# Later scores and per-token-tile round trips in a two-layer decoder trunk, with more transposes taken off TensorE

## The chip, the cores and the metric

The kernel runs on one core of one Trainium2 chip. The metric is device time in microseconds (us). The kernel before takes 1003.44 us, the median of three runs (997.42, 1003.44 and 1008.15). The engines are named as in the profile: PE is TensorE's matmul side and PEld its weight load, DVE is VectorE, ACT is ScalarE, POOL is GpSimd and SP is SyncE. SP and POOL issue most of the DMAs here: SP loads the weights, POOL moves activations out to HBM and back.

## The reference

Two layers on one sequence of 256 tokens and a width of 2048. Each layer normalises x, projects it to q, k, v and a gate z, runs 16 heads' worth of attention in four groups, multiplies by silu(z), projects back and adds x. A last RMSNorm follows.

```python
def _layer_ab(x, norm_g, w_in, w_out, lam_vec, subln_g, layer_idx, pos):
    h = jnp.matmul(_rmsnorm(x, norm_g).astype(x.dtype), w_in).astype(jnp.float32)
...
    ya = _dilated_mixture(_rope(_heads(aq, A_HEADS), pos), _rope(_heads(ak, A_HEADS), pos), _heads(av, A_HEADS))
...
    yb = _diff_attention(bq[:, :, 0], bq[:, :, 1], bk[:, :, 0], bk[:, :, 1], bv, lam)
    yb = _rmsnorm(yb, subln_g) * (1.0 - lam_init)
...
    y = jnp.concatenate([ya, yb], axis=-1) * jax.nn.silu(z)
    return x + jnp.matmul(y.astype(x.dtype), w_out)

def _layer_c(x, norm_g, w_in, w_out, pos):
    h = jnp.matmul(_rmsnorm(x, norm_g).astype(x.dtype), w_in).astype(jnp.float32)
    cq, ck, cv, z = jnp.split(h, [C_WIDTH, 2 * C_WIDTH, 3 * C_WIDTH], axis=-1)
    yc = _moba_attention(_rope(_heads(cq, C_HEADS), pos), _rope(_heads(ck, C_HEADS), pos), _heads(cv, C_HEADS))
    y = _merge(yc) * jax.nn.silu(z)
    return x + jnp.matmul(y.astype(x.dtype), w_out)
```

At 256 tokens the second layer's block attention is plain causal attention. In the first layer, groups 0 and 1 are dilated attention (four heads each) and groups 2 and 3 are differential attention (two heads each, with two score maps and a value width of 256).

## The kernel before, in words

**Tiling.** The tokens are two tiles of 128. Every projection is cut into chunks of 512 output columns: 20 chunks a layer, 40 in all, in the order v q k z for group 0, then q k z v for groups 1 to 3, then four output chunks o. A chunk sums over 16 tiles of the contraction; one such step is called a slot, so a chunk has 16 slots and the kernel 640. In a slot each token tile gets three matmuls of 128x512 in a split-fp32 form: with x and w each cut into a high and a low part, high by high, high by low and low by high (`mm3`, L310). That is six matmuls a slot.

**Feeding.** SP loads the weights 1 MB at a time (four slots, three buffers). For every two slots ACT writes the weights' high part (`wh`, L122) and DVE the low part (`wl`, L123), three pairs ahead and into four buffers. ACT, DVE and POOL each work through their own list in order.

**What lies between the slots.** `at(slot, f, ...)` hangs a piece of work behind a slot's matmuls; the slot numbers are written by hand. A scheduler then orders each engine's list by these priorities and its own times, so the lists can differ a little from the numbers. `nxt` is the slot at which the chunk in question ends.

**Turning.** q, k and the gate come out of a projection as tokens by features and are needed as features by tokens. `evac_rope` (rotary for q and k, five DVE instructions) or `evac_z` works on one token tile; `turn` (L233) transposes 32x32 blocks on DVE; `place` (L238), once both token tiles are turned, stores the 512 KB tile `bz` to HBM (`dt`) and loads it back with eight DMAs (`q`, `k` or `u`), which puts the blocks in place. All of this is on POOL's queue. `split_rope` (L278) then makes the high and low parts, with ACT and DVE (`qh`, `ql`, `kh`, `kl`).

**Attention.** `softmax` (L314) makes scores for a head (`ps_s`), from k, q and their parts. `attn_t` transposes the probabilities the same way over HBM: a store `d` and four loads `p`, on POOL. `attn_h` splits them (`th`, `tl`), and `attn_o` or `diff_o` multiplies by v (`po`, `pdo`). For differential heads `diff_y` transposes the result `yb` on PE (`ps_yt`). `finish_y` multiplies by the gate and splits y (`yh`, `yl`), which the output chunks need.

**Between the layers.** After each output chunk of layer 0, `next_x` (L434) transposes the four 128-wide pieces of the new x on PE (`ps_xt`) and `split_x` splits them for layer 1.

## Time and profile before

| What | Value |
|---|---|
| median of three runs | 1003.44 us |
| profiled execution, whole | 999.49 us |
| its span, first to last instruction | 997.7 us |
| mean granted clock of TensorE | 0.971 |
| PE busy | 942.4 us (94%) |
| DVE busy | 643.0 us (64%) |
| ACT busy | 474.5 us (48%) |
| POOL busy | 200.5 us (20%) |
| PE waiting for k to come back from HBM | 41.6 us, 7 times |

PE's busy time counts pipelined matmuls from start to end, so it is not a measure of full speed; a 128x512 matmul is listed at about 0.39 us, while in a steady stretch one starts every 0.227 us. "Waits" name the engine that waited, what it was about to do, and what ended the wait. The granted clock of a stretch is 1.00 at full speed and 0.50 at half.

### The profile page before, as it was taken

The page shows a single profiled execution, that of the slowest core. Times are in us where ns is not written, and L with a number is a line of the kernel's source. Part 1 is how long each engine was busy: PE and PEld are TensorE (multiplying, and loading weights), DVE is VectorE, ACT ScalarE, POOL GpSimd, SP SyncE. Part 2 cuts the span into 40 slices and gives each one's busy share as a digit, 9 for nine tenths or more (in the row PEclk, how much of TensorE's full clock was granted, in tenths as well). Part 3 has the DMA queues.
Part 4 walks back from the last instruction along what each step waited for, and adds up shares of the span by engine and source line. Part 5 has one row for each costly group of instructions (what it writes and reads, how often), then busy time and mean ns, then how long its engine had stood idle before and what let it go on. Part 6 is the DMA issues. An engine that isn't in the chain of part 4 may idle for free. (4 is left out here: it accounts for less than half of the span.)

```text
span 997.7 us, 11928 instructions
## 1 busy us (share of the span) xinstructions
PE 942.4 (94%) x4276; PEld 778.8 (78%) x4276; DVE 643.0 (64%) x999; ACT 474.5 (48%) x711; POOL 200.5 (20%) x368
## 2 busy tenths in 40 slices
PE   8999997999799988999999999979996999799996
PEld 7887886888688867888888878868885888587886
DVE  6666875756566666665555768747664766575572
ACT  7534643553355335554554454535442644264451
POOL 0021441321113110300000125215011421132000
PEclk9999999999989998999999999989997999899999
DMA  9786776566645664655555668667665756676542
GB/s 329 259 320 232 242 241 212 198 210 244 214 161 210 213 232 137 220 196 174 187 193 185 237 212 266 219 199 234 212 209 180 245 198 211 211 241 227 187 169 84
DMA packets 42827, 213.21 MB, mean 214 GB/s; under 512 B 9040, under 2 KB 9808, under 8 KB 22672
## 3 DMA queue, kind: packets, MB, share of 16 engines
q1 hardware_dynamic: 27504, 175.21, 50.1%
q0 software_dynamic: 14976, 36.20, 11.4%
q10 hardware_dynamic: 288, 1.05, 0.3%
q8 instruction: 33, 0.54, 0.2%
q14 instruction: 26, 0.21, 0.1%
HBM read 192.23 MB, written 20.19 MB: 213 GB/s over the span
## 5 line engine op out<-in xcount | busy, mean ns | idle before, releaser
L312 PE MATMUL acc<-wh,x 128*128 128x512 f32 x2048 | 655.1, 397 | 1.6 <-ACT wh L119 1.6
L123 DVE TENSOR_TENSOR wl<-raw,wh 128x1024 fp32r<-128x1024 f32 x314 | 382.7, 1220 | 206.1 <-ACT wh L122 205.3
L122 ACT ACTIVATE wh<-raw 128x1024 fp32r<-128x1024 f32 x314 | 332.0, 1059 | 359.8 <-PE acc L312 322.2
L312 PEld LDWEIGHTS acc<-wh,x 128*128 128x128 f32 x2048 | 390.7, 191 | 81.9 <-ACT wh L119 1.8
L312 PE MATMUL acc<-wl,x 128*128 128x512 f32 x1024 | 405.1, 396 | 0.2 <-DVE wl L120 0.2
L312 PEld LDWEIGHTS acc<-wl,x 128*128 128x128 f32 x1024 | 196.0, 191 | 39.8 <-DVE wl L120 0.5
L312 PE MATMUL acc<-wh,yh 128*128 128x512 f32 x224 | 88.3, 394 | 0.0
L312 PE MATMUL acc<-wl,yh 128*128 128x512 f32 x224 | 87.4, 390 | 0.0
L312 PE MATMUL acc<-wh,yl 128*128 128x512 f32 x224 | 87.3, 390 | 0.0
L243 POOL DMA_DIRECT2D dt<-bz x24 | 13.6, 568 | 305.6 <-DVE bz L235 302.1
L360 POOL DMA_DIRECT2D p<-d x112 | 61.2, 554 | 56.8 <-DMA d<-bt 29.5
L317 PE MATMUL ps_s<-k,q 128*128 128x128 f32 x64 | 14.7, 315 | 41.8 <-DMA k<-dt 41.6
L317 PEld LDWEIGHTS ps_s<-k,q 128*128 128x128 f32 x64 | 12.8, 214 | 47.0 <-issue 29.8
L312 PEld LDWEIGHTS acc<-wh,yl 128*128 128x128 f32 x224 | 42.0, 188 | 9.1 <-DVE yl L389 0.3
L312 PEld LDWEIGHTS acc<-wl,yh 128*128 128x128 f32 x224 | 42.1, 188 | 8.4
L312 PEld LDWEIGHTS acc<-wh,yh 128*128 128x128 f32 x224 | 42.1, 188 | 8.2
L247 POOL DMA_DIRECT2D q<-dt x64 | 34.7, 550 | 39.2 <-ACT wh L122 19.7
L247 POOL DMA_DIRECT2D k<-dt x64 | 34.7, 549 | 32.6 <-DMA dt<-bz 19.6
L356 POOL DMA_DIRECT2D d<-bt x28 | 15.7, 561 | 124.3 <-DVE st L328 85.6
L247 POOL DMA_DIRECT2D u<-dt x64 | 34.7, 549 | 19.0 <-DMA p<-d 13.2
L286 DVE TENSOR_TENSOR kl<-k,kh 128x512 fp32r<-128x512 f32 x16 | 11.0, 688 | 39.1 <-ACT kh L285 39.1
L285 ACT ACTIVATE kh<-k 128x512 fp32r<-128x512 f32 x16 | 10.0, 624 | 44.3 <-DMA k<-dt 44.2
(122 smaller groups left out, 663.8 us busy)
## 6 DMA issues: line engine op xcount, KB each, us to landing
raw<-in_w SPq DMA_DIRECT2D x124, 1024.0 KB, 5.2
raw<-in_o SPq DMA_DIRECT2D x32, 1024.0 KB, 4.8
dt<-bz POOLq DMA_DIRECT2D x24, 512.0 KB, 4.2
d<-bt POOLq DMA_DIRECT2D x28, 192.0 KB, 4.3
p<-d POOLq DMA_DIRECT2D x112, 48.0 KB, 4.7
q<-dt POOLq DMA_DIRECT2D x64, 64.0 KB, 3.6
k<-dt POOLq DMA_DIRECT2D x64, 64.0 KB, 6.2
u<-dt POOLq DMA_DIRECT2D x64, 64.0 KB, 4.6
```

The lines of the kernel that those rows point to most:

```text
L122: nc.scalar.activation(ht, r, AF.Copy)
L123: nc.vector.tensor_sub(lt, r, ht.bitcast(F32))
L243: nc.gpsimd.dma_start(d, bt.rearrange("p c t h j -> p c (t h j)"))
L247: nc.gpsimd.dma_start(t[32 * c:32 * c + 32, tt].rearrange("p a h j -> p a (h j)"), dv[c, tt])
L285: nc.scalar.activation(a, v, AF.Copy)
L286: nc.vector.tensor_sub(b, v, a.bitcast(F32))
L312: nc.tensor.matmul(out_, l, r, start=start and i == 0, stop=stop and i == 2)
L317: nc.tensor.matmul(ps[:, 0:P], q[:, h * P:(h + 1) * P], k[:, 0, :, h], start=True, stop=True)
L356: nc.gpsimd.dma_start(d, bt.rearrange("p c b j -> p c (b j)"))
L360: nc.gpsimd.dma_start(pt[32 * c:32 * c + 32], dv[c])
```

## The change

Five edits.

1. **By token tile.** `turn` and `place` become one function. Each token tile's turned block is stored by itself (256 KB instead of 512 KB, a `bz` of half the size with two buffers, `dt` with four), as soon as it is turned. With the second one, the eight loads are issued: four for the first token tile, four for the second. The second token tile's rotary or gate work hangs one slot after the first's instead of two.
2. **Later scores.** `split_rope` moves from `nxt + 13` to `nxt + 18`; the first scores move from `nxt + 14` to `nxt + 22`, or to `nxt + 20` in a layer's last group. What follows them moves too; the distance between a head's scores and its product with v becomes shorter.
3. **x of layer 1.** For the first three output chunks of layer 0, `turn_x` and `turned_x` take the same way over DVE, HBM and POOL in place of `next_x`; the last output chunk keeps PE.
4. **y of the third group.** In group 2 of layer 0, `yb` is turned the same way; group 3 keeps PE.
5. **Start.** 13 instead of 10 warm-up matmuls ahead of the first weights.

```diff
-WARM = 10
+WARM = 13
...
+    def turn(src, box, tt, name, into=None):
+        n = src.shape[1]
+        bt = work.tile([P, n], F32, tag="bz", name="bz", bufs=2).rearrange("p (c h j) -> p c h j", c=4, j=32)
+        nc.vector.transpose(bt.rearrange("p c h j -> p h c j"), src.rearrange("p (h c j) -> p h c j", c=4, j=32))
+        d = dram.tile([P, 4, n // 4], F32, tag="dt", name="dt", bufs=4)
+        nc.gpsimd.dma_start(d, bt.rearrange("p c h j -> p c (h j)"))
+        box[tt] = d.rearrange("(a i) c x -> c i a x", a=4)
+        if tt == 1:
+            t = work.tile([P, 2, CW], F32, tag=name, name=name) if into is None else into
+            box["t"] = t = t.rearrange("p t (a h j) -> p t a h j", a=4, j=32)
+            for i in range(2):
+                for c in range(4):
+                    nc.gpsimd.dma_start(t[32 * c:32 * c + 32, i].rearrange("p a h j -> p a (h j)"), box[i][c])
...
+        if g < 3:
+            for tt in range(2):
+                turn(yb[:, tt], box, tt, None, yb)
...
+    def turn_x(n, box, tt):
+        turn(x_sb[:, tt, n * CW:(n + 1) * CW], box, tt, "qk"[n % 2])
+
+    def turned_x(n, h, box):
+        kt = 4 * n + h
+        split_x(1, kt, box["t"][:, :, :, h], xhl[kt].rearrange("p b (t a j) -> p b t a j", t=2, a=4))
...
-                    at(nxt + 2 * tt, evac_rope, ps, kind, (Q, K)[kind == "k"], layer, g, tt, box)
+                    at(nxt + tt, evac_rope, ps, kind, (Q, K)[kind == "k"], layer, g, tt, box)
...
-                at(nxt + 13, split_rope, kind, (Q, K)[kind == "k"], layer, g, box)
+                at(nxt + 18, split_rope, kind, (Q, K)[kind == "k"], layer, g, box)
...
+            late = g == 3
+            first = nxt + (20 if late else 22)
...
-                    at(nxt + 14 + 3 * h, attn_s, layer, g, h, md if layer == 0 else mc, box)
-                    at(nxt + 17 + 3 * h, attn_t, box)
-                    at(nxt + 32 + 2 * h, attn_h, box)
-                    at(nxt + 34 + 2 * h, attn_o, layer, g, h, box)
+                    at(first + 3 * h, attn_s, layer, g, h, md if layer == 0 else mc, box)
+                    at(first + 3 + 3 * h, attn_t, box)
+                    at(first + (13 if late else 15) + 3 * h, attn_h, box)
+                    at(first + (15 if late else 17) + 3 * h, attn_o, layer, g, h, box)
...
+            if layer == 0 and g < 3:
+                box = {}
+                for tt in range(2):
+                    at(nxt + 1 + tt, turn_x, g, box, tt)
+                for h in range(4):
+                    at(nxt + 18 + h, turned_x, g, h, box)
+            elif layer == 0:
```

The differential heads' slots change likewise: their first scores stand at `first` and `first + 5`, and their products with v at `first + 16` and `first + 30` in group 2 and at `first + 16` and `first + 21` in group 3.

How the lists move is shown for group 1 of layer 0. First PE's list around that group's first scores, before: `acc_1330` is the z chunk that follows the k chunk, x_101 is the first tile of the contraction and x_115 and x_116 are its last two, so the first scores stand behind the fifteenth slot of the z chunk.

```order
L312 MATMUL acc_1330<-wh_1425,x_115 128x512 x2
L312 MATMUL acc_1330<-wl_1426,x_115 128x512
L312 MATMUL acc_1330<-wh_1425,x_115 128x512
L317 MATMUL ps_s<-k,q 128x128
L312 MATMUL acc_1330<-wh_1425,x_116 128x512
L312 MATMUL acc_1330<-wl_1426,x_116 128x512
```

Now the same place on PE after the change: `acc_1511` is the next chunk (v), and here x_104 is the first tile of the contraction, so x_110 is its seventh.

```order
L307 MATMUL acc_1511<-wh_1512,x_110 128x512
L312 MATMUL ps_s<-k,q 128x128
L307 MATMUL ps_s<-kh,qh 128x256
L307 MATMUL ps_s<-kl,qh 128x256
L307 MATMUL ps_s<-kh,ql 128x256
L307 MATMUL acc_1511<-wh_1512,x_111 128x512
```

The first scores moved from behind slot 15 after the k chunk's end to behind slot 23, and a head's four products now stand together.

POOL's list for the same group before (q, k and gate round trips, then the four heads' probabilities):

```order
L247 DMA q<-dt 32x4x128 x8
L243 DMA dt<-bz 128x1024
L247 DMA k<-dt 32x4x128 x8
L356 DMA d<-bt 128x384
L243 DMA dt<-bz 128x1024
L360 DMA p<-d 32x4x96 x4
L247 DMA u<-dt 32x4x128 x8
L356 DMA d<-bt 128x384 x2
L360 DMA p<-d 32x4x96 x8
L356 DMA d<-bt 128x384
L360 DMA p<-d 32x4x96 x4
```

And after the change, from the k store on, without the fourth head's store and loads:

```order
L242 DMA dt<-bz 128x512
L249 DMA k<-dt 32x4x128 x4
L242 DMA dt<-bz 128x512
L249 DMA k<-dt 32x4x128 x4
L242 DMA dt<-bz 128x512
L249 DMA u<-dt 32x4x128
L242 DMA dt<-bz 128x512
L249 DMA u<-dt 32x4x128 x7
L351 DMA d<-bt 128x384
L355 DMA p<-d 32x4x96 x4
L351 DMA d<-bt 128x384 x2
L355 DMA p<-d 32x4x96 x8
```

The first four k loads now stand ahead of the second k store, and the gate's whole round trip stands ahead of the first head's store.

ACT's list around the splitting of k before, where `wh` rows feed two slots of PE each:

```order
L122 ACTIVATE wh_1459<-raw_1411 128x1024
L122 ACTIVATE wh_1481<-raw_1445 128x1024
L285 ACTIVATE kh<-k 128x4x128
L122 ACTIVATE wh_1514<-raw_1445 128x1024
L285 ACTIVATE kh<-k 128x4x128
```

And after, where `wh_1459` feeds the v chunk's first two slots and `wh_1493` its fifth and sixth:

```order
L122 ACTIVATE wh_1443<-raw_1390 128x1024
L280 ACTIVATE kh<-k 128x4x128
L122 ACTIVATE wh_1459<-raw_1429 128x1024
L122 ACTIVATE wh_1477<-raw_1429 128x1024
L280 ACTIVATE kh<-k 128x4x128
L122 ACTIVATE wh_1493<-raw_1463 128x1024
```

Counted in weight pairs, the two splits of k moved forward by three pairs and by two on ACT's list, so that they stand ahead of weights that PE needs at slot 16 and at slot 20 after the k chunk's end.

More of the change, by code (lines that the diff above doesn't have):

```diff
@@ L257, in evac_z @@
         nc.vector.scalar_tensor_tensor(z, th, 1.0, z, op0=ALU.add, op1=ALU.mult)
[L258 removed]
+        turn(z, box, tt, "u")
         if tt == 1:
[L260 removed]
+            U[layer, g] = box["t"]
     def evac_rope(ps, name, store, layer, g, tt, box):
[L263 to L264 removed]
         t1 = work.tile([P, CW], F32, tag="t1", name="rt1")
```

62 lines of the change are left out of this document (21 added, 41 removed).

## Prediction

> **What bounds the kernel now.** I read the waits of PE first, since PE is busy for 94% of the span, then the granted clock around the longest of them, then the queue that ends them. Columns of the waits: total us, times, longest.
>
> ```profile
> PE 942.4 (94%) x4276; PEld 778.8 (78%) x4276; DVE 643.0 (64%) x999; ACT 474.5 (48%) x711; POOL 200.5 (20%) x368
> PE ps_s L317 <- DMA k<-dt: 41.6, 7, 7.9
> PE ps_s L312 <- ACT kh L285: 1.8, 2, 1.6
> PE acc L312 <- ACT wh L119: 1.6, 1, 1.6
> PE po L312 <- ACT th L369: 0.5, 1, 0.5
> ```
>
> So PE loses 41.6 + 1.8 = 43.4 us in the middle of the kernel, all of it at a group's first scores; it never waits there for weights. A longer stop costs more than itself. These are stretches of PE (us, its busy time, count, granted clock, share and GB/s of DMA), each begun where PE starts again after such a wait, then two after short waits, then the start of the kernel.
>
> ```profile
> 174.25:181.00 6.75, 6.75 (x24) 0.71 0.08 20
> 274.88:281.00 6.12, 6.12 (x17) 0.53 0.01 2
> 378.04:384.00 5.96, 5.95 (x19) 0.58 0.00 0
> 664.33:671.00 6.67, 6.67 (x20) 0.60 0.04 12
> 767.36:773.00 5.64, 5.64 (x16) 0.58 0.00 0
> 868.92:875.00 6.08, 6.08 (x16) 0.54 0.00 0
> 97.00:107.00 10.00, 9.75 (x47) 1.00 0.49 171
> 592.00:600.00 8.00, 8.00 (x43) 1.00 0.33 137
> 6.60:12.00 5.40, 5.15 (x14) 0.68 1.02 335
> ```
>
> At half clock half the work is lost, so each stretch loses its length times what is missing from 1.00: 6.75 x 0.29 + 6.12 x 0.47 + 5.96 x 0.42 + 6.67 x 0.40 + 5.64 x 0.42 + 6.08 x 0.46 = 15.2 us. With the stops that makes 58.6 us of the 999.49. The two short waits were these, the first with its wait in brackets:
>
> ```profile
> 96.95 0.46 PE L317 MATMUL ps_s<-k,q 128*128 128x128 f32 x2 [1.73 <-DMA k<-dt]
> ```
>
> and the 1.6 of the row for `kh` above; neither cost any clock. The remaining time is PE at full rate, so the change is worth what it takes from these 58.6 and from PE's own list, less the new waits.
>
> Why k is late shows in one group, on PE, POOL and ACT in order of time (start, busy):
>
> ```profile
> 167.95 0.39 PE L312 MATMUL acc<-wh,x 128*128 128x512 f32 x1
> 174.25 0.55 PE L317 MATMUL ps_s<-k,q 128*128 128x128 f32 x1 [5.91 <-DMA k<-dt]
> 161.29 0.56 POOL L243 DMA_DIRECT2D dt<-bz  x1 [15.87 <-DVE bz L235]
> 165.39 4.33 POOL L247 DMA_DIRECT2D k<-dt  x8 [3.55 <-ACT wh L122]
> 187.43 0.55 POOL L243 DMA_DIRECT2D dt<-bz  x1 [1.15 <-DVE bz L235]
> 174.04 0.63 ACT L285 ACTIVATE kh<-k 128x512 fp32r<-128x512 f32 x1 [5.96 <-DMA k<-dt]
> ```
>
> PE stops at 168.2, fifteen slots after the k chunk's end. A steady matmul starts every 0.227 us (rows below), so a slot of six is 1.36 us and the chunk ended at 168.2 - 15 x 1.36 = 147.8. The store is issued 13.5 us after that, and k is there 26.2 us after it (174.04), where the scores wanted it at 20.4.
>
> **The change part by part. Later scores.** They now stand 23 slots after the chunk's end, or 21 in a layer's last group: 31.3 or 28.6 us. When is k there? DVE turns the second token tile no later than before, since its rotary work hangs one slot earlier, so I take the old 13.5 us for its store. The first four loads stand between the two stores and belong to the first; after the second store only four are left, not eight, which takes half of the 4.33 us row, 2.2 us, off the end. So k is whole at 26.2 - 2.2 = 24.0 us at the latest. Spare: 7.3 us, or 4.6 in a last group. The two waits of 43.4 us go, and with them the 15.2 us of half clock.
>
> **By token tile, store size.** DMA from issue to landing, us (median; the last rows min, median, max of p, d and of one load's issue on POOL in ns):
>
> ```profile
> dt<-bz POOLq DMA_DIRECT2D x24, 512.0 KB, 4.2
> d<-bt POOLq DMA_DIRECT2D x28, 192.0 KB, 4.3
> p<-d POOLq DMA_DIRECT2D x112, 48.0 KB, 4.7
> DMA to landing us min/median/max: 2.1/4.7/8.1
> DMA to landing us min/median/max: 2.1/4.3/6.6
> L247 POOL DMA_DIRECT2D k<-dt x64: 548/548/557, 91.6 to 866.1; - x64
> ```
>
> A store of 192 KB lands no sooner than one of 512 KB, so the halved stores gain nothing in landing and each costs one more issue of 0.56 us on POOL. The Trainium skill says otherwise ("DMA: Bandwidth & Descriptors", Anatomy of one DMA): about 2.0 us plus the bytes over 436 GB/s, by which 256 KB less would land some 0.6 us sooner, an estimate; the spare above would be 7.9 and 5.2 us and the sum the same. No run here shows that slope.
>
> **Transposes off PE.** Four of them and what they do to their neighbours:
>
> ```profile
> 436.10 0.39 PE L312 MATMUL acc<-wh,yl 128*128 128x512 f32 x1
> 436.33 0.60 PE L439 MATMUL ps_xt<-ident,x_sb 128*128 128x128 f32 x4
> 436.69 0.48 PE L312 MATMUL acc<-wh,yh 128*128 128x512 f32 x1
> 437.00 0.40 PE L312 MATMUL acc<-wl,yh 128*128 128x512 f32 x1
> ```
>
> The four take 0.36 us and the matmul after them 0.31 instead of 0.23: 0.45 us. Six calls of `next_x` and two of `diff_y` leave PE: 8 x 0.45 = 3.6 us. In return DVE gets six 128x512 and four 128x256 block transposes and POOL ten stores and forty loads. Both have room: POOL is 20% busy, and DVE idles for a third of the span. The x of the third chunk is the tight one. Its turn is issued two slots after the chunk, its loads end about 4.2 (store) + 4.4 (eight issues) + 4.7 us later, some 17 us after the chunk's end with DVE's own work, and layer 1 needs it 24 slots after (32.6 us). But ACT takes that split between two weight pairs, and the next pair is due at 18 slots, 24.5 us; four splits of 0.47 and a weight pair (both in the rows below) end near 21.6. I put nothing down for it.
>
> **Warm-up.** Ten warm-up matmuls (two passes each) end before PE's 1.6 us wait for the first weights; three more fit into it, at 3.95/10 = 0.4 us each.
>
> ```profile
> 1.06 3.95 PE L137 MATMUL pw<-ones 128*128 128x128 f32 x20 [1.06 <-DVE fs L463]
> ```
>
> The stretch from 6.6 us loses 5.40 x 0.32 = 1.7 us at half clock. Filling the pause gains between 0 and 1.7; I take 0.8.
>
> **What the change newly makes PE wait for.** Three places, since the round trips now hang more closely on what needs them. The rows: the weight splits, ACT's wait for p, the splits of p and x, and a differential head's last score and its store.
>
> ```profile
> L123 DVE TENSOR_TENSOR wl<-raw,wh 128x1024 fp32r<-128x1024 f32 x314 | 382.7, 1220 | 206.1 <-ACT wh L122 205.3
> L122 ACT ACTIVATE wh<-raw 128x1024 fp32r<-128x1024 f32 x314 | 332.0, 1059 | 359.8 <-PE acc L312 322.2 <-issue 22.7 <-DMA raw<-in_o 3.4
> ACT th L369 <- DMA p<-d: 16.0, 10, 2.7
> L369 ACT ACTIVATE th<-p 128x256 fp32r<-128x256 f32 x24 | 9.7, 405 | 8.0 <-DMA p<-d 8.0
> L370 DVE TENSOR_TENSOR tl<-p,th 128x256 fp32r<-128x256 f32 x24 | 10.1, 419 | 3.5 <-ACT th L369 3.4
> L152 ACT ACTIVATE x<-ps_xt,g_sb 128x256 fp32r<-128x256 f32 x16 | 7.5, 470 | 10.5 <-DVE x L153 7.5 <-PE ps_xt L439 2.9
> 282.79 0.29 PE L312 MATMUL ps_s<-kh,ql 128*128 128x256 f32 x1
> 289.39 0.56 POOL L356 DMA_DIRECT2D d<-bt  x1 [18.68 <-DVE bt L354]
> ```
>
> First, ACT works in order, and the second split of k now stands ahead of the weights that PE needs 20 slots after the chunk's end, 27.2 us. With k at 24.0, the split (0.63), the weight pair (1.06, 1.22) end at 26.9. It holds, by 0.3 us, on the late bound; a slow landing shows on PE. I take 0.3 us for each of eight groups, 2.4. Second, POOL's three hops. The gate's round trip is ahead of the first head's store: its store stood at 187.43, 39.6 us after the k chunk, or 31.7 without the 5.9 us stop and the 2.0 us of half clock; one slot earlier now, 4.2 to land and four loads make the first head's store leave at about 37. Store and four loads are 6.5 us, the next pair 4.3 + 4.4, the fourth store 0.6, then 4.3 + 2.2 and 4.2 to land: 26.5 us later, 63.5, plus 0.85 for the splits. Regular groups want it at 49 slots, 66.6 us: no wait. In the last group of layer 1 the list is two stores, eight loads, twice over; the third head's part is split at 58.3 us and wanted at 42 slots, 57.1: 1.3 us with the hand-over. Third, differential heads keep 14 slots (19.0 us) from the second scores to the product. The scores take about 0.5, their softmax 6.6 (282.79 to 289.39), store, loads and landing 4.3 + 2.2 + 4.2, and the splits about 1.1, an estimate for half as many columns again as in the rows: 18.9. No spare, so I take 0.6 us for three of the four heads, 1.8. Together 5.5 us. The bounds: 0.5, PE's wait for `th` before, and 8 x 2.7 = 21.6, if every group shows the longest wait of ACT for p.
>
> **The sum**, against the profiled execution: 999.5 - 43.4 - 15.2 - 3.6 - 0.8 + 5.5 = 942.0 us. The median of the runs shown is 3.9 us above that execution; the runs spread by 10.7 us, and the waits that spread go, so I don't add it.
>
> **The rivals.** *The weights become the wait.* k, x and the probabilities block ACT and DVE, which are in order, and PE stops for `wh` in every group. For: the 0.3 us above, and the 2.7. Against: DVE idles 206.1 us and ACT 359.8 in front of the weight splits, and before no such stop exists. Price: 21.6 in place of 5.5 gives 958; if in three groups it also trips the clock, at 2.5 us each (15.2/6), 966. The rows show half clock after the stop of 5.9 us and none after 1.7; between these two no row is shown. The Trainium skill ("TensorE: Matmul & The Clock Gate", Part 1) puts the window at about 3.4 us, by which most of these waits would keep the clock.
>
> *The scores still wait.* The first loads stand ahead of the second store, so a slow first landing delays it, and k with it. It would have to come 7.3 us later than reckoned. Half of the waits left, with their clock, is 29 us: 971.
>
> *Slower: POOL's hops.* If the round trips of a group take long, the fourth head is late in every group. Three hops at the longest landings (6.6 and 8.1 for 4.3 and 4.7) add 17.1 us, less 2.2 of spare (66.6 - 64.4): 14.9 a group, and 2.5 of clock, 139 us over eight groups: 1076. It turns slower than before when a group loses 57.5/8 = 7.2 us beyond the 5.5, so at about 2.3 us more on each of three hops. For: 74 more DMAs on POOL. Against: a load's issue takes 548 to 557 ns throughout, and 4.7 and 4.3 are medians over the same hops in the kernel before. The Trainium skill ("SBUF — State Buffer", "SBUF: two separate sides", the box on DVE blocking DMA) states that certain DVE instructions keep POOL from writing a DMA's descriptors; by that rule more DVE work beside more POOL DMAs would go this way. The issue row doesn't show it, with DVE 64% busy.
>
> **How the numbers follow.** The forecast has 0.73, the weights' wait 0.14, scores that still wait 0.05, slower 0.04; the other 0.04 are cases in which the gains and new waits nearly cancel. Predicted 942. The likeliest case reaches from 934 (new waits 0.5, the start's full 1.7, a lighter execution by 2) to 952; the range goes on to 962, into the first rival, and 3 us below, as landings vary from run to run. About 1% is what a measurement of this kernel can tell from no change: 993 to 1013. Faster 0.92, same 0.04, slower 0.04.
>
> **What would show it.** PE's wait for k gone or under 5 us; the mean granted clock above 0.99 instead of 0.971; no `ps_xt` behind the first three output chunks; a span near 940. The weights' rival shows as waits of PE for `wh` or `wl`, POOL's as waits of PE for `th` or `tl` behind p, the second as k in PE's waits. The forecast is wrong if any of these comes to more than 20 us.

## The result, and the profile after

The changed kernel takes 971.15 us (median of four runs, 967.66 to 975.80) against 1000.43 us for the kernel before on the same chip (997.42 to 1008.15): 0.970 of it, with an interval of 0.963 to 0.977. The profiled execution takes 967.66 us, its span 965.9 us, and the mean granted clock rose from 0.971 to 0.987. The forecast said 942.0 and reached up to 962. So the direction holds, and nearly half of the gain is missing.

First the page's row of the engines, then the waits of PE (total us, times, longest) and of ACT:

```profile
PE 931.3 (96%) x4250; PEld 771.5 (80%) x4250; DVE 648.2 (67%) x1009; ACT 468.9 (49%) x711; POOL 242.7 (25%) x442
```

```profile
PE po L307 <- ACT th L364: 8.8, 2, 6.3
PE acc L307 <- DVE wl L123: 4.2, 7, 1.2
PE ps_yt L420 <- DVE yb L407: 2.4, 1, 2.4
PE acc L307 <- ACT wh L122: 2.3, 2, 1.8
PE pdo L307 <- ACT th L364: 1.6, 2, 1.0
PE po L307 <- DVE y L381: 1.3, 1, 1.3
...
ACT kh L280 <- DMA k<-dt: 55.8, 16, 7.3
ACT th L364 <- DMA p<-d: 47.5, 16, 8.1
```

No row of PE names k any more: the 43.4 us before the first scores are gone. In their place stand six kinds of short stops. ACT, which stopped 16.0 us for p before, now stops 47.5. All pauses of PE over 0.3 us in this trace, from the end of the first chunk on, add up to 20.1 us. Four of the places are followed by half clock (stretch, PE's busy time and count, granted clock, DMA share, GB/s):

```profile
158.20:163.20 5.00, 4.98 (x14) 0.50 0.59 198
415.80:419.20 3.40, 3.40 (x10) 0.50 0.64 214
494.30:497.70 3.40, 3.40 (x10) 0.50 0.81 287
634.30:637.70 3.40, 3.40 (x12) 0.50 0.69 234
```

That is (5.0 + 3 x 3.4) x 0.5 = 7.6 us. With the forecast's other terms left as they were, 999.5 - 43.4 - 15.2 - 3.6 - 0.8 + 20.1 + 7.6 = 964.2, which is 3.5 us short of the measured 967.7. The term for new waits was 5.5 and came out at 27.7 us: 13.0 where group 0's fourth heads wait for `th` (6.28 and 2.48 us, with 2.5 and 1.7 of clock), 5.7 in layer 0's first output chunk, 5.5 behind the splits of the turned x, and 3.6 in small stops elsewhere in layer 0's group 0.

The missing 3.5 us lie behind the last matmul, where the forecast has no term: from there to the end of the span the kernel before takes 7.9 us and the changed kernel 12.1. The rows of POOL's closing instruction DRAIN give its duration in ns (shortest, median, longest of three) and when the first and the last of the three start; the longest is the first one, behind POOL's last arithmetic. Before, then after:

```profile
L630 POOLq DRAIN  x3: 40/102/3903, 991.2 to 997.4; - x3
L645 POOLq DRAIN  x3: 40/102/9945, 955.1 to 965.6; - x3
```

Before, it ended 2.7 us ahead of the span's end, and SP's wait for the output rows ended last. After, SP is through 5.1 us ahead of the end, and the closing rows of all engines start when POOL's DRAIN is over. In all 18 profiles of this case its length goes by the number of DMAs that POOL has issued: 3.90 us with 356 of them, 5.86 with 380, 7.50 with 400, 8.31 with 410 and 9.95 with 430, so about 0.082 us each. The changed kernel issues 74 more than the kernel before. Its DRAIN is 6.0 us longer, and 4.2 us of these show at the end. With these the sum is 968.4, within 1 us of the measurement.

The largest of the new waits, in three engines of the changed kernel (start, busy, in brackets the idle time before and what ended it): POOL, ACT and PE at the fourth head of group 0.

```profile
136.62 0.56 POOL L351 DMA_DIRECT2D d<-bt  x1
139.00 0.57 POOL L249 DMA_DIRECT2D q<-dt  x1 [1.82 <-ACT th L364]
...
145.82 2.18 POOL L249 DMA_DIRECT2D q<-dt  x4 [2.50 <-DMA dt<-bz]
147.99 1.09 POOL L355 DMA_DIRECT2D p<-d  x2
...
150.71 0.55 POOL L355 DMA_DIRECT2D p<-d  x1 [0.90 <-DMA q<-dt]
```

```profile
154.21 0.63 ACT L280 ACTIVATE qh<-q 128x512 fp32r<-128x512 f32 x1 [6.71 <-DMA q<-dt]
...
156.82 1.04 ACT L122 ACTIVATE wh<-raw 128x1024 fp32r<-128x1024 f32 x1
157.77 0.40 ACT L364 ACTIVATE th<-p 128x256 fp32r<-128x256 f32 x1
```

```profile
158.22 0.58 PE L307 MATMUL po<-th,vh 128*128 128x256 f32 x1 [6.28 <-ACT th L364]
```

The head's store (`d<-bt`) leaves at 136.62, but its loads (`p<-d`) only at 147.99 to 150.71: in POOL's list all eight loads of the next q stand ahead of them, and four of those wait for q's second store. The store had landed at 138.96; the last load landed at 155.63. ACT adds to it: in its list the split of q (`qh`), which waited for q until 154.1, and a weight half stand ahead of `th`, so `th` starts 2.1 us after its data is there (0.3 us in layer 1). Of the stop of 6.28 us some 4 belong to the late loads and 2 to ACT's list. The Trainium skill ("DMA: Bandwidth & Descriptors", Anatomy of one DMA — SWDGE (gpsimd) path) states that a wait on a semaphore happens on the issuing sequencer before the DMA is sent; the 2.50 us in which POOL stands in front of q's loads, with p's behind them, agree.

### The profile page after: what moved, and what is told of

Read it like the earlier page. It is cut to its first block, busy times and chain, and to the rows that moved or that the text cites. A ratio compares the mean times of both kernels' runs of the same rounds, so it can differ in the third digit from the quotient of the medians.

```text
span 965.9 us, 12042 instructions
## 1 busy us (share of the span) xinstructions
PE 931.3 (96%) x4250; PEld 771.5 (80%) x4250; DVE 648.2 (67%) x1009; ACT 468.9 (49%) x711; POOL 242.7 (25%) x442
## 3 DMA queue, kind: packets, MB, share of 16 engines
q1 hardware_dynamic: 27504, 175.21, 51.7%
## 4 chain that ended last, share of the span: by engine, by line
PE 51%; issue 13%; DMA 10%; POOL 4%; DVE 3%; ACT 2%; ACTq 0%; POOLq 0%; DVEq 0%
PE acc L307 48%; DMA dt<-bz 4%; DMA d<-bt 2%; DMA p<-d 2%; POOL q L249 1%; PE last L480 1%; DVE wl L123 1%; POOL k L249 1%; ACT wh L122 1%; DMA k<-dt 1%; PE po L307 1%; DMA q<-dt 1%; PE ps_s L307 1%; POOL p L355 1%; POOL u L249 0%
## 5 line engine op out<-in xcount | busy, mean ns | idle before, releaser
L307 PE MATMUL acc<-wh,x 128*128 128x512 f32 x2048 | 647.6, 393 | 2.2 <-ACT wh L122 1.8
L307 PEld LDWEIGHTS acc<-wh,x 128*128 128x128 f32 x2048 | 386.7, 189 | 82.5 <-ACT wh L122 3.0
L122 ACT ACTIVATE wh<-raw 128x1024 fp32r<-128x1024 f32 x314 | 327.5, 1054 | 217.3 <-PE acc L307 195.5
L242 POOL DMA_DIRECT2D dt<-bz x58 | 33.0, 569 | 285.5 <-DVE bz L240 285.2
L249 POOL DMA_DIRECT2D q<-dt x80 | 43.8, 554 | 66.3 <-DMA dt<-bz 49.6
L249 POOL DMA_DIRECT2D k<-dt x72 | 39.3, 552 | 74.7 <-DMA dt<-bz 41.3
L321 ACT ACTIVATE p<-p,st 128x128 f32<-128x128 f32 x64 | 28.5, 446 | 32.8 <-DVE st L317 32.8
L364 ACT ACTIVATE th<-p 128x256 fp32r<-128x256 f32 (+1 forms) x28 | 12.0, 428 | 50.0 <-DMA p<-d 47.5
L365 DVE TENSOR_TENSOR tl<-p,th 128x256 fp32r<-128x256 f32 (+1 forms) x28 | 12.3, 440 | 24.8 <-ACT th L364 24.8
```

The source lines that it names most:

```text
L122: nc.scalar.activation(ht, r, AF.Copy)
L242: nc.gpsimd.dma_start(d, bt.rearrange("p c h j -> p c (h j)"))
L249: nc.gpsimd.dma_start(t[32 * c:32 * c + 32, i].rearrange("p a h j -> p a (h j)"), box[i][c])
L307: nc.tensor.matmul(out_, l, r, start=start and i == 0, stop=stop and i == 2)
L321: nc.scalar.activation(p[:, sl], p[:, sl], AF.Exp, bias=st[:, 0, i:i + 1], scale=-1.0, accum_out=st[:, 1, i:i + 1])
L364: nc.scalar.activation(th4, pt[:, 0:n], AF.Copy)
```

## The experiments

Medians of one kernel differ by up to 1.3% from one measurement to another (`g0_list` below: 973.58 and 960.93 us on two chips), so the places are compared too. The table gives stretches of PE's timeline in each profiled execution, from the first matmul of one chunk to the first of a later one (chunks counted from 0, in the order v q k z, q k z v three times, four output chunks, then the second layer), in us; in brackets PE's pauses of over 0.3 us inside it. Half clock after a pause is in the stretch, not in the bracket. All pauses are counted from chunk 1 on; the end is the time from the last matmul to the end of the span.

| Kernel | 5 to 7 | 13 to 15 | 15 to 17 | 17 to 21 | 26 to 27 | 31 to 33 | 35 to 37 | all pauses | end |
|---|---|---|---|---|---|---|---|---|---|
| before | 54.3 (5.9) | 53.2 (7.7) | 49.7 (0) | 90.9 (0) | 29.3 (5.6) | 49.4 (0) | 51.7 (0.9) | 44.0 | 7.9 |
| changed | 59.2 (9.1) | 44.6 (0) | 56.2 (4.0) | 94.5 (3.8) | 26.8 (2.5) | 47.7 (0) | 48.9 (0) | 20.1 | 12.1 |
| changed_again | 58.1 (9.0) | 51.9 (4.4) | 49.4 (0) | 90.9 (1.9) | 27.1 (3.0) | 47.7 (0) | 50.8 (1.3) | 22.3 | 12.1 |
| late_alone | 48.5 (1.7) | 45.6 (0) | 52.0 (1.2) | 90.9 (0) | 24.8 (2.1) | 52.8 (3.4) | 60.5 (6.7) | 26.7 | 7.9 |
| tiles_alone | 49.0 (1.6) | 45.5 (0.8) | 48.4 (0) | 90.9 (0) | 22.9 (0) | 49.6 (0.4) | 49.0 (0.9) | 23.2 | 8.0 |
| x_on_pe | 54.1 (4.8) | 49.6 (3.1) | 56.5 (4.5) | 90.9 (0) | 27.6 (3.3) | 49.3 (0.8) | 49.7 (0.8) | 21.0 | 9.6 |
| g0_early | 49.9 (2.8) | 48.6 (2.2) | 55.5 (4.0) | 91.5 (2.7) | 22.4 (0) | 50.7 (1.7) | 49.8 (0.9) | 19.5 | 12.1 |
| g0_list | 50.9 (3.6) | 51.6 (5.3) | 55.2 (2.7) | 94.5 (5.2) | 22.8 (0) | 54.5 (4.2) | 50.5 (1.2) | 23.6 | 12.1 |
| g0_early_again | 50.1 (1.9) | 47.0 (2.1) | 58.5 (6.1) | 95.0 (4.4) | 22.4 (0) | 49.9 (0.8) | 49.4 (0) | 18.9 | 12.1 |
| g0_list_again | 52.4 (4.5) | 45.9 (0.9) | 57.3 (4.7) | 93.2 (3.6) | 23.4 (0.8) | 48.2 (0) | 49.2 (0) | 15.2 | 12.1 |
| u_stores_first | 55.1 (6.2) | 46.6 (1.7) | 50.2 (0.5) | 92.2 (3.1) | 29.5 (4.2) | 47.7 (0) | 48.5 (0) | 17.5 | 12.1 |
| y_on_pe | 55.6 (7.1) | 45.6 (0) | 55.4 (3.3) | 94.0 (3.2) | 25.3 (2.6) | 53.4 (3.5) | 50.1 (1.1) | 22.8 | 10.5 |
| u_and_y | 56.2 (7.3) | 45.6 (0) | 49.4 (0) | 94.6 (3.7) | 29.9 (4.7) | 49.3 (0.8) | 52.3 (1.7) | 21.1 | 10.4 |
| three_mended | 50.9 (2.7) | 51.7 (4.9) | 49.4 (0) | 90.9 (0) | 22.4 (0) | 47.7 (0) | 56.1 (3.7) | 16.3 | 9.6 |
| three_mended_y_on_pe | 49.8 (2.8) | 46.3 (0.5) | 49.8 (0) | 90.9 (0) | 22.4 (0) | 47.7 (0) | 55.6 (4.4) | 10.0 | 8.0 |
| mended_all_stores_first | 48.8 (2.2) | 45.6 (0) | 49.4 (0) | 90.9 (0) | 22.4 (0) | 47.7 (0) | 49.3 (0.4) | 8.4 | 8.0 |
| mended_x_later | 49.5 (2.8) | 45.6 (0) | 49.4 (0) | 96.0 (3.4) | 22.4 (0) | 47.7 (0) | 52.4 (2.9) | 11.4 | 9.6 |
| x_held | 49.2 (2.1) | 45.6 (0) | 49.4 (0) | 89.0 (0) | 22.4 (0) | 47.7 (0) | 49.8 (0.8) | 5.8 | 9.6 |

### Which half of the first two edits makes the gain

`late_alone`: the kernel before with the changed kernel's whole table of slots; its single 512 KB store and all transposes on PE stay.

```diff
-at(nxt + 13, split_rope, ...)
+at(nxt + 18, split_rope, ...)
-at(nxt + 14 + 3 * h, attn_s, ...)
+at(first + 3 * h, attn_s, ...)
...
```

> The kernel before with one part of the change alone: the new table of slots (evacuation in adjacent slots, the split at the 18th slot, the scores from the 20th or 22nd, the heads' turns and products as in the change). The turned q, k and gate still leave in one store of 512 KB each, all transposes stay on TensorE, and 10 warm-up matmuls. Theory A (the later scores are the whole gain, the stores by token tile add next to nothing since a store of half the size lands in 4.3 us against 4.2): TensorE waits for k and kh under 3 us in all, eight more transposes (3.6 us) stay and the waits behind the turned x (5.5 us) don't come: 960 to 972 us, ratio 0.963 to 0.972. Theory B (the scores can be met only because the first token tile's store leaves early): k lands 2 to 4 us later in each of eight groups, TensorE waits 16 to 30 us for k, ratio 0.98 to 1.00.

`tiles_alone`: the changed kernel with the whole table of the kernel before, all transposes on PE and 10 warm-up matmuls; the stores by token tile stay.

```diff
-at(first + 3 * h, attn_s, ...)
+at(nxt + 14 + 3 * h, attn_s, ...)
...
```

> The kernel before with the other half of the first part alone: the turned q, k and gate leave in two stores, one for each token tile, and the loads for each token tile hang on its own store; the table of slots is the one before (evacuation two slots apart, split at the 13th slot, scores from the 14th), all transposes on TensorE, 10 warm-up matmuls. Theory A (the later scores are the gain, a halved store lands no sooner): TensorE still waits 35 to 45 us for k and kh, 995 to 1005 us, ratio 0.99 to 1.005. Theory B (the first tile's earlier store is a good part of the gain): k's last load lands 2 to 4 us sooner in each of eight groups, the waits fall to 15 to 25 us, and with the half clock that follows the ratio is 0.97 to 0.985. Theory C (the second store stands behind the first tile's loads in POOL's list): k lands later than before, and the time grows by 5 to 15 us.

Measured: `late_alone` 974.75 us, 0.969 (0.963 to 0.975); `tiles_alone` 974.24 us, 0.968 (0.961 to 0.976). Each half alone gives what the whole change gives. Waits of PE, and one kind of DMA (KB each, median us to landing), of `tiles_alone`, then of `late_alone`:

```profile
PE ps_s L307 <- ACT kh L280: 18.1, 7, 5.8
PE ps_s L307 <- DVE kl L281: 1.9, 6, 0.3
...
dt<-bz POOLq DMA_DIRECT2D x48, 256.0 KB, 3.9
```

```profile
PE po L312 <- ACT th L369: 7.9, 4, 2.8
PE po L312 <- DVE y L387: 5.3, 5, 1.7
...
PE ps_s L312 <- ACT kh L285: 2.2, 1, 2.2
...
dt<-bz POOLq DMA_DIRECT2D x24, 512.0 KB, 4.0
```

`tiles_alone` follows its theory B: the waits for k fall from 43.4 to 20.0 us. Half a store lands no sooner, 3.9 us against 4.0; but only four loads instead of eight have to wait for the second store. From the end of the second tile's block transpose to k's last landing it takes 11.5 us on the mean of eight groups, against 14.3 before and 14.7 in `late_alone`. Four issues less are 2.2 us of this difference; and the gain is one of the mean: in two of the eight groups k came hardly sooner than before or later (13.7 against 13.9 us, 15.7 against 13.8). `late_alone` follows its theory A: hardly any wait for k (2.6 us with `kl`), but other waits of PE come up, for `th`, `y` and the weight halves, and its pauses add up to 26.7 us. So there are two ways to the same 0.97. That the later scores, put on top of the stores by token tile, take away the rest of the wait for k, and that the closer table behind them gives about as much back, is argued from these waits: the two halves together without edits 3 to 5 were not run, and in the changed kernel 4.1 us of the end come on top.

### The places where the time is given back

`x_on_pe`: edit 3 undone; all output chunks go through `next_x`.

```diff
-            if layer == 0 and g < 3:
+            if layer == 0 and g in ():
...
             elif layer == 0:
                 at(nxt + 3, next_x, g, 0)
```

> The changed kernel with the second layer's x of all four column chunks turned on TensorE again; all else as changed. Theory A (the turned x is a loss: ScalarE stops in its order for it and the weight halves queue behind): the four waits of TensorE behind the x splits (0.54, 0.76, 1.75, 0.77 us) and one stretch of half clock (1.7 us) go, 24 transposes (2.7 us) come back, and the stretch from the first output chunk's end to the second layer's start (94.5 us now, 90.9 before the change) falls to about 91: some 3.5 us, 0.4% less, 0.966 of the kernel before instead of 0.970. Theory B (the transposes cost TensorE more than the waits): the stretch stays at 94 us or grows, and the ratio is 0.970 to 0.975. Theory C (the prediction's 942 was missed because of these transfers above all): 10 us or more go, ratio 0.96 or less.

Measured: 972.8 us, 0.968 (0.960 to 0.975). The stretch from 17 to 21 falls from 94.5 to 90.9 us, which was theory A's number; but the next profile of the unaltered kernel has 90.9 there too, with 1.9 us of pauses, so the loss at this place is 0 to 3.6 us. The end is 2.4 us shorter, with 30 DMAs less on POOL. In the changed kernel ACT stands at x's splits in its list, and the weight halves stand behind them:

```profile
465.05 1.71 ACT L153 ACTIVATE x<-k,g_sb 128x256 fp32r<-128x256 f32 x4 [7.61 <-DMA k<-dt]
489.89 1.71 ACT L153 ACTIVATE x<-q,g_sb 128x256 fp32r<-128x256 f32 x4 [8.83 <-DMA q<-dt]
```

The total could not show a gain of this size.

`g0_early`: the scores of group 0 two slots earlier, so that POOL's list has the fourth head's loads before the next q.

```diff
-            first = nxt + (20 if late else 22)
+            first = nxt + (20 if late else 20 if g == 0 else 22)
-at(first + (13 if late else 15) + 3 * h, attn_h, ...)
+at(first + (13 if late else 17 if g == 0 else 15) + 3 * h, attn_h, ...)
...
```

> The changed kernel with the scores and the first half of the heads' turn of group 0, in both layers, two slots earlier (scores from the 20th slot after k's chunk instead of the 22nd), so that the fourth head's four loads of p stand ahead of the next q's stores and loads in POOL's list; the products stay at their slots. Theory A (in group 0 the fourth head's p stands behind the next q's round trip on POOL): the waits for th of 6.28 us and of 2.48 us ahead of the fourth head's products go, with the half clock behind each (3.4 and 1.7 us): about 13 us less, 0.957 of the kernel before instead of 0.970. Theory B (p's own round trip is too long wherever it stands): the waits stay at 2 us or more, and the time within 3 us of the changed kernel's. Theory C (the earlier scores are too early for k): TensorE waits for k or kh at group 0's first score, 1 to 5 us each, and half of the gain goes.

`g0_list`: the order of the list, with the scores and products left where they are. The eight loads of group 1's q are tied behind the last load of p issued so far; `behind_p` is true for that q alone. For that the fourth head's turn hangs one slot earlier.

```diff
+            if behind_p and tt == 1:
+                es.enter_context(tc.issue_after(last_p[-1]))
-at(first + 3 + 3 * h, attn_t, box)
+at(first + 3 + 3 * h - (g == 0 and h == 3), attn_t, box)
```

> The changed kernel with POOL's list alone put otherwise in group 0 of both layers: the next q's eight loads stand behind the fourth head's four loads of p (whose turn is traced one slot earlier for that); the scores and the products stay at their slots, unlike the earlier run that moved the scores too. Theory A (the order of POOL's list is the cause): p's loads of the fourth head are issued some 6 us sooner, and the waits for th ahead of its products (6.28 and 2.48 us in the changed kernel, 5.09 and 4.18 us with the gate's stores first) fall under 1 us with the half clock behind them: 8 to 14 us less, ratio 0.955 to 0.962. Theory B (the two slots of time did it): the waits stay above 2 us and the ratio near 0.970. q's own loads land 2 to 3 us later; nobody waits for q before its k.

Measured: `g0_early` 956.03 us, 0.952 (0.945 to 0.958); `g0_list` 973.58 us, 0.968 (0.960 to 0.975), on another chip. In both the long waits for `th` are gone and the stretches 5 to 7 and 26 to 27 are 8 and 4 us shorter or more. But the list edit's total did not fall: in its profile pauses of 5.3, 5.2 and 4.2 us stand at three places which the edit does not touch. So both ran again on one chip:

> The changed kernel with group 0's scores two slots earlier, again, beside the list edit on one chip. Theory A (both edits take the same waits away): no wait for th over 1.5 us in group 0; ratio within 0.007 of the list edit's, both 0.955 to 0.965. Theory B (the two slots do more than the list): at least 0.010 less than the list edit's.

> The changed kernel with POOL's list alone put otherwise in group 0, again. Theory A: no wait for th over 1.5 us in group 0, the stretches 5 to 7 and 26 to 27 within 1.5 us of the earlier scores' (49.9 and 22.4 us), ratio 0.955 to 0.965. Theory B (q's loads, later by four loads of p, push a wait to ScalarE's split of q and so to the weight halves): waits for wh or wl of over 2 us in the stretches behind group 0 (chunks 7 to 8, 27 to 28), ratio 0.965 to 0.972.

Measured: 963.06 us, 0.961 (0.953 to 0.968), and 960.93 us, 0.958 (0.950 to 0.965). The stretches are 50.1 and 22.4 us with the earlier scores, 52.4 and 23.4 with the list. Theory A holds in the main: with p's loads ahead of q's in POOL's list the long waits go, and the two slots are not needed for it. `th` also stands ahead of q's split on ACT then, so the two lists are not told apart by these runs; the landings above put some 4 of the 6.28 us on POOL. Two details missed their bounds: the stretch 5 to 7 is 2.5 us longer than the 49.9 named, not 1.5 at most, and a stop of 1.68 us stays at the fourth head's product. The profile names DVE's `y` for it, which stands in DVE's list behind `tl`; `tl` waits for `th`, and `th` for p, whose loads, issued at once, still take 4.8 to 8.0 us to land. POOL and ACT of `g0_list_again`:

```profile
141.81 0.54 POOL L245 DMA_DIRECT2D dt<-bz  x1 [3.95 <-DVE bz L243]
142.34 2.20 POOL L363 DMA_DIRECT2D p<-d  x4
144.53 1.63 POOL L257 DMA_DIRECT2D q<-dt  x3
```

```profile
152.08 0.42 ACT L372 ACTIVATE th<-p 128x256 fp32r<-128x256 f32 x1 [5.25 <-DMA p<-d]
```

`u_stores_first`: the gate's second store (`st`) ahead of the eight loads; `STORES_FIRST` is `("u",)`.

```diff
+            with ExitStack() as es:
+                if name in STORES_FIRST:
+                    es.enter_context(tc.issue_after(st.ins))
                 for i in range(2):
...
```

> The changed kernel with the gate's two stores issued one behind the other, ahead of all eight of its loads, instead of the second store behind the first load. Theory A (in POOL's list the second store waits until the first has landed, 2.3 to 2.6 us after its data is there): the gate's last load lands 2 to 4 us sooner in each of the eight groups, in the last group of the first layer the first head's store leaves POOL 2 us or more sooner than 1.5 us after its turn, and the waits of TensorE in the first output chunk (0.58, 1.03 and 2.35 us, and 1.7 us of half clock) shrink to under 2 us in all: 3 to 4 us less, 0.966 of the kernel before. Theory B (those waits hang on the heads' own chain: scores, softmax, two hops): no wait there changes by more than 0.5 us, and the ratio stays 0.970. Theory C (the list before was hiding the stores' time): the time grows.

Measured: 964.49 us, 0.960 (0.953 to 0.967). POOL around the gate of layer 0's last group, in the changed kernel and then in `u_stores_first`:

```profile
372.67 0.56 POOL L242 DMA_DIRECT2D dt<-bz  x1 [7.49 <-DVE bz L240]
377.00 0.56 POOL L249 DMA_DIRECT2D u<-dt  x1 [3.77 <-DMA dt<-bz]
377.55 0.56 POOL L242 DMA_DIRECT2D dt<-bz  x1
378.10 1.64 POOL L249 DMA_DIRECT2D u<-dt  x3
383.44 2.17 POOL L249 DMA_DIRECT2D u<-dt  x4 [3.69 <-DMA dt<-bz]
```

```profile
372.78 0.56 POOL L243 DMA_DIRECT2D dt<-bz  x1 [7.31 <-DVE bz L241]
375.65 0.56 POOL L243 DMA_DIRECT2D dt<-bz  x1 [2.30 <-DVE bz L241]
378.75 4.37 POOL L253 DMA_DIRECT2D u<-dt  x8 [2.54 <-DMA dt<-bz]
```

One load ahead of the second store holds it until the first store has landed. Over eight groups the gate is whole 8.9 us after its last transpose instead of 14.0, more than the 2 to 4 us expected. The stretch 15 to 17 falls from 56.2 to 50.2. But that stretch also has 49.4 us in the next profile of the unaltered kernel, so that part of the gain is not always there to be had. Group 0's waits are still there, 5.09 and 4.18 us.

`changed_again`: the changed kernel, unaltered.

> The changed kernel itself, unaltered, for a second profiled execution. Theory A (the waits found are the kernel's own): again waits for th ahead of the fourth head's products in group 0 of both layers (6.28 and 2.48 us in the first profile), a stop of over 2 us at the transposes of y in the first output chunk, two stops behind the x splits; each within 3 us of the first profile; time 966 to 976 us. Theory B (they are luck of one execution): two or more of these places show no wait over 1 us. In the 14th and 15th chunk, where the first profile shows no wait and three runs with small edits elsewhere show 1.7 to 5.3 us for wl, theory A' (y's eight loads stand among the next q's there, and how long ScalarE stops at q's split is a matter of landings) expects a wait of 1 to 5 us in this execution, theory B' none.

Measured: 972.78 us, 0.973 (0.966 to 0.980). Group 0's waits are there again, 6.19 and 3.02 us: they belong to the kernel. The stops in the first output chunk are not there; a stop of 4.40 us that the first profile lacks is:

```profile
360.02 0.80 PE L307 MATMUL acc<-wl,x 128*128 128x512 f32 x1 [4.40 <-DVE wl L123]
```

```profile
355.83 0.42 ACT L382 ACTIVATE yh<-y 128x256 fp32r<-128x256 f32 x1 [5.59 <-DVE y L381]
...
357.41 2.93 ACT L122 ACTIVATE wh<-raw 128x1024 fp32r<-128x1024 f32 x3
```

```profile
338.15 2.21 POOL L249 DMA_DIRECT2D q<-dt  x4 [4.24 <-DMA dt<-bz]
340.35 1.11 POOL L242 DMA_DIRECT2D dt<-bz  x2
347.34 4.36 POOL L249 DMA_DIRECT2D yb<-dt  x8 [5.88 <-DMA dt<-bz]
```

So theory A holds for group 0, and in smaller size for the x splits (0.39 and 0.76 us), and B for the output chunk. At the stop of 4.40 us ACT waits for y, whose two stores and eight loads stand behind q's loads on POOL, not for q as the expectation had it.

### Edit 4, and all places together

`y_on_pe` undoes edit 4; `u_and_y` does so on top of `u_stores_first`; `three_mended` has x on PE, the earlier scores of group 0 and the gate's stores first; `three_mended_y_on_pe` adds the undone edit 4.

```diff
-        if g < 3:
+        if g < 2:
             for tt in range(2):
                 turn(yb[:, tt], box, tt, None, yb)
...
-        if g == 3:
+        if g >= 2:
             pt = patt.tile([P, 2, S], F32, tag="T", name="ps_yt")
```

> The changed kernel with y of the third group turned on TensorE as before the change, nothing else. Theory A (y by way of the memory costs a wait for wl behind q's split in the 14th and 15th chunk in most executions): the stretch from the 10th to the 15th chunk under 113 us without a wait over 1 us there, and the median 2 to 6 us less than the changed kernel's: ratio 0.963 to 0.968. Theory B (the transposes were worth moving): 8 of them back, 0.9 us more, ratio 0.970 to 0.972; a wait in that stretch is then there all the same.

> The changed kernel with three of its places put otherwise at once: x on TensorE for all column chunks, the scores of group 0 two slots earlier, the gate's two stores ahead of its loads. If the three losses are separate places, as the profiles have them, the gains add up: 0.970 less 0.018 less 0.010 less 0.003, a ratio of 0.937 to 0.945, about 940 us, and TensorE waits under 10 us in all. If they cover for each other (a later arrival turns up at the next wait), less: 0.945 to 0.952.

> The run with three places mended, and y of the third group on TensorE as before the change as well. Theory A (y by way of the memory costs nothing but POOL's time): 8 transposes come back, 0.9 us more, and no wait goes: the stretch from the 11th to the 15th chunk 0.9 us longer. Theory B (y's stores and loads stand among the next q's on POOL, q's split stops ScalarE, and the weight halves queue behind it; waits of 3.10, 2.23 and 1.68 us for wl stood in that stretch in three of the runs): the stretch gets 1 to 4 us shorter, and the ratio falls by 0.001 to 0.004.

> The changed kernel with the gate's stores ahead of its loads and y of the third group on TensorE. Theory A (y's eight loads among the next q's cost a wait for wl in chunks 13 to 15; the gate's order hid it before): that stretch 45.6 us (46.6 with the gate's stores alone), no wait over 1 us there, nor in chunks 31 to 33, ratio 0.952 to 0.960. Theory B (y by way of the memory is neutral): 0.960 or more, as with the gate's stores alone.

Measured: `y_on_pe` 975.69 us, 0.978 (0.970 to 0.986); `three_mended` 961.42 us, 0.954 (0.946 to 0.962); `three_mended_y_on_pe` 949.14 us, 0.943 (0.936 to 0.950); `u_and_y` 969.19 us, 0.966 (0.959 to 0.972). At its place y behaves as theory A of `y_on_pe` said: with y on PE the stretch 13 to 15 is 45.6, 46.3 and 45.6 us with pauses of 0.5 at most; with y by way of HBM it is 45.9 to 51.9 us, and 44.6 in the first profile alone. The totals show it only in the pair of the two `three_mended` kernels, which ran on one chip (1.1% apart, with intervals that just overlap). `y_on_pe` and `u_and_y` came out no faster than the kernels without it; in their profiles pauses of 3.5 us in 31 to 33, or of 7.3 and 4.7 at group 0, stand against it. What edit 4 alone costs in the total stays open; of its 20 DMAs the end shows 1.6 us (12.1 against 10.5), more than the 0.9 us that its eight transposes take on PE. And `three_mended` did not reach the sum of the single gains, 0.937 to 0.945, while a wait at y was left in it.

### Two more steps

`mended_all_stores_first`: as `three_mended_y_on_pe`, and `STORES_FIRST = ("u", "k", "q")`.

> The run with three places mended and y on TensorE, and k's and q's second stores ahead of all their loads too, as the gate's. Theory A (ScalarE's stops at the splits of k and q, which hold up the weight halves, are shortened): k's last load lands 9 us after its data is there instead of 10.9, the waits for wh and wl (6.6 us in the run without this) fall to 3 us: ratio 0.937 to 0.943. Theory B (all landings are hidden now, and the waits left are behind p's): no change, 0.943. Theory C (the first tile's loads landing early hid half of the split): ScalarE stops longer, 0.944 to 0.950.

`mended_x_later`: that, and x of the first two output chunks by way of HBM with `turned_x` at `nxt + 25`.

> As the run with all stores first, but x of the first two column chunks by way of the memory as in the change, with its splits from the 25th slot after the chunk instead of the 18th; the third and fourth on TensorE. Theory A (x waits only because its split is early: 15.6 us from the store to the last landing, 11.5 slots, and ScalarE runs some 7 slots ahead of TensorE): no stop at the x splits over 1 us, 16 transposes (1.8 us) gone: 0.002 less than the run beside it. Theory B (the transfers disturb the weights' stream or the last gate's): waits of 1 us or more in the output chunks, and the ratio 0 to 0.004 more.

`x_held`: the same, with the splits tied behind the last weight half traced.

```diff
-        split_x(1, kt, ...)
+        with tc.issue_after(last_wh[0]):
+            split_x(1, kt, ...)
```

> The run with three places mended, y on TensorE and all second stores first, with x of the first two column chunks by way of the memory and its splits held behind later weight halves in ScalarE's list (seven pairs later than where the changed kernel has them; the earlier run with later slots left them in place). Theory A (only the place of the split in ScalarE's list made x wait): no stop over 1 us behind the x splits, 16 transposes fewer (1.8 us): the stretch from the 17th to the 21st chunk 89.1 us instead of 90.9, ratio 0.940 to 0.946. Theory B (the 16 loads and stores disturb the weights' stream, or the last gate and the next layer's start): waits of 1 us or more there, stretch 91 to 95 us.

Measured: 945.57 us, 0.947 (0.941 to 0.952); 954.29 us, 0.955 (0.949 to 0.962); 946.13 us, 0.945 (0.939 to 0.950). Stores first for k and q change nothing (theory B): k is whole 11.5 us after its transpose, against 11.2 without. `mended_x_later` did not do what it says: the splits stood behind the same weight half in ACT's list as in the changed kernel, although their slot is seven later. A later slot alone does not hold an instruction back; why the build's scheduler left it there is not shown. So x waited as before:

```profile
451.94 1.31 ACT L154 ACTIVATE x<-k,g_sb 128x256 fp32r<-128x256 f32 x3 [8.98 <-DMA k<-dt]
```

With the splits held seven pairs later, ACT does not wait for x at all, and the stretch 17 to 21 takes 89.0 us; 89.1 was expected. So at its place x by way of HBM pays its 1.8 us once its split stands late enough. But its 20 DMAs more make the end 1.6 us longer (9.6 against 8.0), and next to nothing is left: the totals are 945.57 without it and 946.13 with it, on two chips. All waits of PE in `x_held`:

```profile
PE acc L311 <- DVE wl L124: 5.0, 8, 1.5
PE po L311 <- DVE y L385: 1.2, 1, 1.2
PE pw L138 <- DVE fs L473: 1.1, 1, 1.1
PE po L311 <- ACT th L368: 0.8, 1, 0.8
PE acc L311 <- DVE wl L121: 0.2, 1, 0.2
```

Three versions, `three_mended_y_on_pe`, `mended_all_stores_first` and `x_held`, cannot be told from one another by their totals. At 0.943 to 0.947 all three beat both kernels.

## Why the prediction was half right

**Later scores: right.** The 43.4 us of waits for k went entirely. k was there in time: in the six groups without a long stop of PE in between, its last load landed 20.3 to 25.4 us after the chunk's end (in the second layer's third group 745.6 against 725.2). The 24.0 that the prediction put as the latest was passed by up to 1.4 us, and the spare of 7.3 us covered that. The runs add that the two halves overlap: the later scores alone take 40.8 of the 43.4 us, the stores by token tile alone 23.4. The step "store size" was right about the landing; what the smaller stores gain is four loads fewer behind the second one, which the forecast had taken in as 2.2 us of spare.

**Half clock: right in kind, not complete.** The stretches behind k's waits went, but 7.6 of 15.2 us came back behind four new stops.

**New waits: the step that failed, 5.5 us against 27.7.** Its count of POOL's three hops took the list of a regular group, where nothing but the gate and the heads stands on POOL. In group 0 of each layer the next chunk is q, and "Regular groups want it at 49 slots, 66.6 us: no wait" does not hold there; two groups cost 13.0 us. The 1.3 us of the second layer's last group came out as pauses of 0 and 1.3 us in the two profiles. "I put nothing down" for x was wrong by 5.5 us in one profile and about 2 in the other. The landing was mis-sized: the third chunk's x was reckoned at some 17 us after the chunk's end and came at 25.0 and 22.1 us in the two profiles. In the first its turn was ready only some 9 us after the chunk's end, since DVE had stood 6.9 us at the second chunk's split; the stores took 5.6 to 5.9 us instead of 4.2, and the loads 5.8 to 7.3 instead of 4.7. ACT reached the split 16.7 us after the chunk's end, so it stood there for 8.8 us, with the weight halves behind it. "No spare, so I take 0.6 us" for the differential heads named the place; it was worth 4.0 us of pauses in one execution and none in the other. And y of the third group had no term of its own for a wait; its stretch, 13 to 15, is 7.3 us longer in the second profile than in the first.

**Split of k ahead of the weights.** The 0.3 us a group did not show in the changed kernel's own two profiles between 31 and 33, but 3 to 4 us did in `late_alone`, `g0_list` and `y_on_pe`. There k's last load landed 30.9, 31.0 and 28.4 us after the chunk's end, against 20.4 and 23.2 in the changed kernel's two profiles: 24.0 was not the latest, and the spare was small.

**Transposes, and what POOL pays for them: a term put at nothing.** With x held, 16 transposes less take 1.9 us (90.9 to 89.0), so 0.45 us for four is right, and the changed kernel has 32 transposes less on PE (4250 matmuls against 4276, with six passes more of warm-up). What failed is "Both have room: POOL is 20% busy". Of 74 more DMAs on POOL, 50 are those of edits 3 and 4, and POOL's closing DRAIN grows with each: the end is 4.2 us longer. In `tiles_alone`, with the 24 stores of edit 1 alone, it is 0.1 us longer, since its DRAIN of 5.86 us is still nearly covered by SP's wait. So edits 3 and 4 give back at the end some 4.1 us, which is about what they take from PE.

**Warm-up.** Chunk 1, the second, starts between 30.2 and 31.0 us in all profiles, 10 or 13 matmuls alike: the 0.8 us is not shown.

**The rivals.** "The weights become the wait" (958 to 966) came near in size, and ACT's stops in its list are its mechanism; but the largest price was POOL's list, the mechanism of the "slower" rival, at two groups instead of eight. "The scores still wait" names the time, 971, and not the cause; that the time fits is luck. No rival had the end. Of the signs that the prediction named, the clock above 0.99 and the span near 940 did not come, yet none of the waits passed its 20 us, because the loss is spread over several places. With the places mended the kernel takes 945.6 and 946.1 us, with 8.4 and 5.8 us of pauses. That is near 942, but not by the forecast's sum: in the first all transposes are back on PE, and in the second the end takes what x by way of HBM saves.

## What to carry to other kernels

When a round trip through memory is moved closer to its use, read the in-order list of the issuing queue at every place where the sequence of work is irregular, not only in the regular period: the price here was two groups out of eight. A DMA whose data is ready can stand behind one that waits, so stores belong ahead of loads that wait for another store. Count the DMAs of a queue as well as its busy share: here each one more on POOL lengthened the end of the kernel by 0.08 us once the output rows no longer covered it. And an early place in an engine's list is as harmful as a late landing: what must wait should stand where its data is there, tied down if a scheduler orders the list.

## What was not expected of the hardware

A store of 512 KB and one of 256 KB land alike (4.0 and 3.9 us in the two half edits, 4.2 and 4.3 before and after).

POOL's closing DRAIN takes 3.90 to 9.95 us, by the number of DMAs that POOL issued: among the 18 profiles it differs by less than 0.01 us where the numbers are equal, whatever else the kernels do differently. Why it goes by this number is not shown.

The length of a stop alone does not decide on the clock. This stop of 2.35 us in the changed kernel was followed by half clock (the row of 415.80 above), the one of 2.59 us in `y_on_pe` was not:

```profile
414.51 0.74 PE L420 MATMUL ps_yt<-ident,yb 128*128 128x128 f32 x4 [2.35 <-DVE yb L407]
```

```profile
634.31 0.39 PE L307 MATMUL po<-th,vh 128*128 128x256 f32 x1 [2.59 <-ACT th L364]
```

```profile
634.40:637.60 3.20, 3.20 (x17) 1.00 0.39 97
```

The clock records of the profiles show why. Every half-clock stretch between the first chunk and the last matmul lasts 3.41 or 6.83 us, or 10.24 in the kernel before (three times), and in each of the 12 executions that have several they start at whole multiples of 3.413 us from one another: in the changed kernel at 156.41, 415.82, 494.33 and 634.28, which are 76, 23 and 41 such steps. If the span of all 17 profiles with such a stretch is cut on this grid, every window at full clock in which PE paused for 2.0 us or more is followed by half clock, and none in which it paused for less than 1.5; between 1.5 and 1.9 both occur. The stop of 2.35 us lay with 2.1 us in one window; that of 2.59 us was cut into 1.7 and 0.9. So the stretch between 1.7 and 5.9 us that the prediction left open closes at 1.5 to 2.0 us of pause within one window. The Trainium skill ("TensorE: Matmul & The Clock Gate", Part 1) states a free-running window of about 3.4 us, and the grid agrees; its rule of thumb, that only pauses over about 3.4 us matter, does not: some half of a window is enough here.

And the waits move between executions of one kernel: the same place cost 4.4 us or nothing, while the total stayed within 1%. A single profile told which waits were possible, and only the second told which belonged to the kernel.
